# A conditioned two-layer trunk: four chunks of the conditioning product in a row, and VectorE's block transposes in place of selection matmuls

## The chip, the cores and the metric

One core of one Trainium2 chip runs the whole program. The metric is the time of one execution on the device in microseconds (us), as the median of several runs. The engines are TensorE (PE, with its weight loads PEld), VectorE (DVE), ScalarE (ACT), GpSimd (POOL) and SyncE (SP), which here only issues DMAs.

## What is computed

Two layers over 256 prompt tokens and 8 x 4 sample tokens of 1024 features. Each layer is a feed-forward, a mixer (a recurrence beside pooling) and a second feed-forward. All three are normalized and modulated by conditioning vectors, nine in number (one for the prompt, eight for the samples):

```python
mod = (jax.nn.silu(c) @ w_mod[l] + b_mod[l]).reshape(Bn, 3 * N_SUB, D_MODEL)[:, None]
u = _modnorm(x, norm_g[l, 0], mod[:, :, 0], mod[:, :, 1])     # rmsnorm(x, g) * (1 + scale) + shift
x = x + 0.5 * mod[:, :, 2] * _swiglu(u, w_ffn_in[l, 0], w_ffn_out[l, 0])
...
```

The mixer uses slots 3, 4 and 5 in the same way, the second feed-forward 6, 7 and 8.

`silu(c) @ w_mod[l]` is the conditioning product: 9 rows by 1024 by 9216 columns for each layer, 72 MB of weights in all. Its result is wanted with the features on the partitions: `mod[l]` is [128, 72 feature tiles, 9].

## The kernel before

Activations lie with the features on the partitions and 288 tokens on the free axis. A float32 product is three float32r passes, so a weight tile of 128x128 gives three matmuls of 288 columns (`mm3`, L243). Weights come from memory in slots of eight tiles (`load_slot`, L203, 512 KB, three buffers, issued on SP). Each half slot, a strip of four tiles, is split by ScalarE (`wh`, L224) and VectorE (`wl`, L225) into buffers for four strips. A feed-forward (`ffn`, L516) first makes 22 pairs of column tiles (gate and up, index j, 16 weight tiles each) and then 8 output tiles (22 weight tiles each). The first pairs behind a norm take a special form; `first_products` covers them.

The conditioning product is woven in between. A chunk is one load of 1 MB (`modw`, L292, SP's queue, five buffers). Its matmuls (L314) use four column tiles of TensorE at once: block q of the chunk's columns goes to partitions 32 q of a PSUM tile `psmd`, of which there is one buffer. A wide chunk holds 128 rows of `w_mod` for 4 x 512 columns. So a large group of 2048 columns takes eight chunks; the tail of each layer (1024 columns) takes four chunks, and the first layer's first 2048 columns are four small groups of two chunks each, in which a chunk holds 512 rows for 4 x 128 columns. `mod_step` (L296) carries out one chunk. `ffn` calls it at the head of every pair j from 3 or 4 on (L584) and behind every output tile (L600), with two loads ahead; below, such a place is called a tick. Groups 0 to 6 of layer 0 are opened at the program's start, 36 more chunks (layer 0's tail, layer 1's large groups) at the end of the first mixer, and layer 1's tail at the end of the second (L1299). `mod_close` flushes what is left at a mixer's head.

When a group is complete, ScalarE copies its PSUM rows to SBUF (L321). The next `mod_step` first calls `mod_cols` (L324): a matmul per 128 columns of `rows` against the constant `sel` (L334) brings the nine wanted rows of each block to the features' partitions, and VectorE adds the bias and finishes shifts, scales and gates (L341, L347, L351). These matmuls write `psmd` too (`pswk` for the small groups).

The order of instructions on each engine is set at build time by the framework's planner. It takes, of the instructions that its own model of time thinks ready, the one that was written first; blocks under `high_priority` (weight loads and splits) count as written 75 instructions earlier. The weight tiles' matmuls are tied to each other in their written order by `issue_after`; the conditioning product's matmuls are not, except in the first 48 weight tiles.

Of the kernel before, what the change touches and what calls it, by code (L numbers as in the profile page):

```python
# [25 lines left out]
P = 128  # L26
# [21 lines left out]
NV = NT + NC9 + 1  # even, as float32r asks  # L48
# [4 lines left out]
# w_in's column tiles in the order in which the mixer wants them: lora, k, r, v, gate lora, pool.  # L53
# [19 lines left out]
# behind a norm: pairs of column tiles (feed-forward) and column tiles (mixer) that don't wait for it  # L73
# [3 lines left out]
# w_mod's columns in groups of four blocks (one to a column tile of the tensor engine): the blocks'  # L77
# width and first columns. A chunk is one load of a group's rows. The first layer's first groups are
# the shifts and scales of two feature tiles each: its first products start behind them.
MODC = 2048  # L80
MOD_TAIL = [(256, [8192 + 256 * q for q in range(4)])]
MOD_GROUPS = [
    [(128, [256 * h + o for o in (0, 128, 1024, 1152)]) for h in range(4)]
    + [(512, [2048 * g + 512 * q for q in range(4)]) for g in range(1, 4)] + MOD_TAIL,
    [(512, [2048 * g + 512 * q for q in range(4)]) for g in range(4)] + MOD_TAIL,
]
MOD_CHUNKS = [[D * 4 * w // (P * MODC) for w, _ in g] for g in MOD_GROUPS]
# [100 lines left out]
class Kernel:  # L188
# [135 lines left out]
    def mod_cols(self):  # L324
        """Brings a finished group's rows to the features' partitions."""
        nc = self.nc
        if self.mod_rows is None:
            return
# [4 lines left out]
        for j in range(nj):  # L333
            nc.tensor.matmul(ps[:, 36 * j:36 * j + 36], rows[:, P * j:P * j + P], self.cst("sel"), start=True, stop=True)  # L334
# [1143 lines left out]
```

## Time and profile before

| | us |
|---|---|
| median of 3 runs | 1487.39 (1486.8 to 1488.97) |
| span of the profiled execution | 1486.2 |
| TensorE busy in it | 1438.0 |
| VectorE busy | 937.8 |
| ScalarE busy | 725.8 |

The profile is of one execution. Busy times are of the whole span, so they are averages over stages; matmuls are pipelined, so the distance between the starts of two of them tells more than the time given for one. In a chain of waits the program is followed back from its end to what released each step.

### The profile page before, as it was taken

Reading aid. Unit: us, or ns where it says so; the run is one execution under the profiler, and the core shown is the slowest. Engines: PE = TensorE matmul, PEld = TensorE weight load, DVE = VectorE, ACT = ScalarE, POOL = GpSimd, SP = SyncE. Lnnn points to the kernel's source line nnn. Section 1 sums busy time; section 2 is a strip of 40 time slices with the busy share of each in tenths; the row PEclk is TensorE's granted clock in tenths of the full one; section 3 lists DMA queues with packets and bytes.
Section 4 is the critical chain, followed back from the end, with each engine's and each line's share of the span. In section 5 each row is a group of like instructions: output and inputs, shape, how many; then the busy total and the mean of one; then the engine's idle time right before and its main releaser. Section 6 shows DMA issues by size and latency. Waiting matters only on the chain.

```text
span 1486.2 us, 30239 instructions
## 1 busy us (share of the span) xinstructions
PE 1438.0 (97%) x11944; PEld 1311.5 (88%) x11944; DVE 937.8 (63%) x1975; ACT 725.8 (49%) x1456; POOL 222.0 (15%) x320
## 2 busy tenths in 40 slices
PE   6999999999999989999999999999899999999997
PEld 5888899988778988888989899998887799999997
DVE  4544456798656885445567455668966678755554
ACT  4444444674434554444446445447653355645532
POOL 0000001153213130000111000121622213100011
PEclk9999999998999999999999999999999999999999
DMA  8888754443324657777775644443323356444442
GB/s 349 310 322 308 275 183 146 147 136 104 104 76 161 238 189 271 285 265 258 251 256 186 239 139 164 170 168 136 123 89 105 103 178 255 142 156 170 162 166 103
DMA packets 72383, 281.95 MB, mean 190 GB/s; under 512 B 9584, under 2 KB 11504, under 8 KB 62896
## 3 DMA queue, kind: packets, MB, share of 16 engines
q1 hardware_dynamic: 66384, 272.24, 51.3%
q10 hardware_dynamic: 5856, 7.78, 1.6%
q8 instruction: 93, 1.52, 0.4%
q14 instruction: 50, 0.41, 0.1%
HBM read 275.76 MB, written 4.23 MB: 188 GB/s over the span
## 4 chain that ended last, share of the span: by engine, by line
PE 83%; DVE 10%; issue 2%; DMA 1%; POOL 1%; ACT 1%; POOLq 0%; DVEq 0%; SPq 0%; ACTq 0%
PE psmm L250 41%; PE pswk L250 29%; PE psmd L314 4%; DVE wl L225 3%; DVE ul L474 1%; DVE xn L471 1%; DMA modw<-in_wmod 1%; POOL pw L669 1%; PE pswk L1128 1%; PE pswk L896 1%; PE psmd L334 0%; PE pswk L383 0%; PE pswk L1249 0%; DMA cc<-in_c 0%; PE pswk L1030 0%
## 5 line engine op out<-in xcount | busy, mean ns | idle before, releaser
L225 DVE TENSOR_TENSOR wl<-raw,wh 128x512 fp32r<-128x512 f32 x732 | 520.4, 714 | 411.6 <-ACT wh L224 402.4
L224 ACT CAST wh<-raw 128x512 fp32r<-128x512 f32 x732 | 452.1, 620 | 573.4 <-PE psmm L250 297.1
L250 PE MATMUL psmm<-uh,wh 128*128 128x288 f32 x1072 | 327.2, 305 | 1.1 <-ACT uh L482 1.1
L250 PE MATMUL psmm<-uh,wl 128*128 128x288 f32 x1072 | 319.1, 298 | 4.0 <-DVE wl L225 4.0
L250 PE MATMUL psmm<-ul,wh 128*128 128x288 f32 x1072 | 318.8, 297 | 0.1
L250 PEld LDWEIGHTS psmm<-uh,wh 128*128 128x128 f32 x1072 | 203.7, 190 | 34.4 <-ACT wh L224 19.5
L250 PEld LDWEIGHTS psmm<-uh,wl 128*128 128x128 f32 x1072 | 203.3, 190 | 9.8 <-DVE wl L225 5.1
L250 PEld LDWEIGHTS psmm<-ul,wh 128*128 128x128 f32 x1072 | 203.6, 190 | 2.7 <-issue 1.4
L250 PE MATMUL pswk<-uh,wh 128*128 128x288 f32 x608 | 182.0, 299 | 0.0
L250 PE MATMUL pswk<-ul,wh 128*128 128x288 f32 x608 | 179.9, 296 | 0.0
L250 PE MATMUL pswk<-uh,wl 128*128 128x288 f32 x608 | 179.8, 296 | 0.0
L370 POOL TENSOR_TENSOR sq<-x 128x288 f32<-128x288 f32 x42 | 30.4, 723 | 874.6 <-DVE x L510 866.5
L250 PEld LDWEIGHTS pswk<-uh,wh 128*128 128x128 f32 x608 | 114.7, 189 | 19.2 <-ACT wh L224 18.0
L250 PEld LDWEIGHTS pswk<-uh,wl 128*128 128x128 f32 x608 | 114.6, 189 | 1.7 <-issue 1.7
L250 PEld LDWEIGHTS pswk<-ul,wh 128*128 128x128 f32 x608 | 114.7, 189 | 0.8 <-issue 0.8
L250 PE MATMUL psmm<-hl,wh 128*128 128x288 f32 x352 | 104.0, 296 | 0.0
L250 PE MATMUL psmm<-hh,wh 128*128 128x288 f32 x352 | 104.0, 295 | 0.0
L250 PE MATMUL pswk<-hl,wh 128*128 128x288 f32 x352 | 103.9, 295 | 0.0
L250 PE MATMUL pswk<-hh,wh 128*128 128x288 f32 x352 | 103.9, 295 | 0.0
L250 PE MATMUL pswk<-hh,wl 128*128 128x288 f32 x352 | 103.8, 295 | 0.0
L250 PE MATMUL psmm<-hh,wl 128*128 128x288 f32 x352 | 103.8, 295 | 0.0
L314 PE MATMUL psmd<-modw,csilu 128*32 128x512 f32 (+2 forms) x832 | 79.0, 486 | 9.5 <-DMA modw<-in_wmod 9.5
(340 smaller groups left out, 2513.7 us busy)
## 6 DMA issues: line engine op xcount, KB each, us to landing
raw<-in_wflat SPq DMA_DIRECT2D x366, 512.0 KB, 3.3
modw<-in_wmod SPq DMA_DIRECT2D x72, 1024.0 KB, 5.6
s<-in_wkv ACTq DMA_DIRECT2D x16, 256.0 KB, 2.9
o_wkvs<-s SPq DMA_DIRECT2D x8, 256.0 KB, 2.5
x<-in_x SPq DMA_DIRECT2D x1, 1152.0 KB, 5.8
o_y<-yo SPq DMA_DIRECT2D x2, 288.0 KB, 2.4
o_y<-yo ACTq DMA_DIRECT2D x2, 288.0 KB, 2.6
o_pool<-po SPq DMA_DIRECT2D x8, 67.5 KB, 2.4
```

Of the source, the lines that this page charges most:

```text
L224: self.nc.scalar.copy(wh, src)
L225: self.nc.vector.tensor_tensor(out=wl, in0=src, in1=wh.bitcast(F32), op=ALU.subtract)
L250: self.last = self.nc.tensor.matmul(ps, w, x, start=start and n == 0, stop=stop and n == 2)
L314: mm = nc.tensor.matmul(self.mod_ps[32 * q:32 * q + 32, :size], self.csilu[:, k, :], w[:, kk, q, :], start=(k == 0), stop=(k == KD - 1))
L370: nc.gpsimd.tensor_tensor(out=t, in0=x, in1=x, op=ALU.mult)
L471: nc.vector.scalar_tensor_tensor(out=t, in0=self.x[:, k, :TP], scalar=g1, in1=r[:, :TP], op0=ALU.mult, op1=ALU.mult)
L474: nc.vector.scalar_tensor_tensor(out=ul, in0=t, scalar=s[:, k, 0:1], in1=uh.bitcast(F32), op0=ALU.add, op1=ALU.subtract)
L669: G.tensor_tensor(out=nx[:, lo:], in0=cur[:, lo:], in1=cur[:, lo - d:PEXT - d], op=ALU.add)
L896: T.transpose(ps[:n, 128 * hp:128 * hp + 128], src(hp), ident)
L1128: T.matmul(ps[halves[e], :], BKTs[halves[e], hp, :], uv[halves[e]].rearrange("p b v -> p (b v)"), start=True, stop=True)
```

## The change

Four things are done. First, the feed-forward's ticks call `mod_tick`: it carries out four chunks one behind the other once four of a group are loaded (`MOD_RUN`), and otherwise none; each tick asks for one more load. Second, the columns of `w_mod` are packed differently on the host, before the launch: block q of a group now holds the q-th 32 features of each of the group's feature tiles. Third, `mod_cols` has no matmul: VectorE transposes the group's PSUM tile in blocks of 32x32 straight into `rows`, which puts the 128 features of each tile on the partitions, and the bias is added from there. It is called directly behind a group's last chunk. Fourth, ScalarE's copy and the constant `sel` are gone. Comments and docstrings are left out of the new file.

```diff
 MODC = 2048
-MOD_TAIL = [(256, [8192 + 256 * q for q in range(4)])]
+MOD_BUFS, MOD_RUN = 5, 4
 MOD_GROUPS = [
-    [(128, [256 * h + o for o in (0, 128, 1024, 1152)]) for h in range(4)]
-    + [(512, [2048 * g + 512 * q for q in range(4)]) for g in range(1, 4)] + MOD_TAIL,
-    [(512, [2048 * g + 512 * q for q in range(4)]) for g in range(4)] + MOD_TAIL,
+    [[2 * h + o for o in (0, 1, 8, 9)] for h in range(4)]
+    + [list(range(16 * g, 16 * g + 16)) for g in range(1, 4)] + [list(range(64, 72))],
+    [list(range(16 * g, 16 * g + 16)) for g in range(4)] + [list(range(64, 72))],
 ]
...
     def mod_step(self, n=1):
         nc = self.nc
         for _ in range(n):
-            self.mod_cols()
             if self.mod_at == len(self.mod_todo):
                 return
-            self.mod_load(int(self.mod_ahead == 0))
+            self.mod_load(int(self.mod_ahead == 0 and self.mod_next == self.mod_at))
...
             self.mod_load()
             if nk * (c + 1) == KD:
-                rows = self.p_rows.tile([P, 512], F32, tag="rows", name="rows")
-                nc.scalar.copy(rows[:, :size], self.mod_ps[:, :size])
-                self.mod_rows = rows, l, size, starts
-
-    def mod_cols(self):
-        """Brings a finished group's rows to the features' partitions."""
+                self.mod_cols(l, tiles, size)
+
+    def mod_tick(self):
+
+        if self.mod_at == len(self.mod_todo):
+            return
+        l, g, c = self.mod_todo[self.mod_at]
+        n = min(MOD_RUN, MOD_CHUNKS[l][g] - c)
+        if self.mod_next - self.mod_at >= n:
+            self.mod_ahead = 0
+            self.mod_step(n)
+        self.mod_ahead = self.mod_next - self.mod_at
+        self.mod_load(1)
+
+    def mod_cols(self, l, tiles, size):
+
         nc = self.nc
...
-        nj = size // P
-        ps = self.ps_wk() if nj == 1 else self.p_md.tile([P, 512], F32, tag="md", name="psmd")
-        for j in range(nj):
-            nc.tensor.matmul(ps[:, 36 * j:36 * j + 36], rows[:, P * j:P * j + P], self.cst("sel"), start=True, stop=True)
-        pv = ps[:, :36 * nj].rearrange("p (j q c) -> p q j c", j=nj, q=4)
...
+        rows = self.p_rows.tile([P, 512], F32, tag="rows", name="rows")
+        nc.vector.transpose(rows[:, :size], self.mod_ps[:, :size])
+        rows = rows[:, :size].rearrange("p (m r) -> p m r", r=32)
+        n = 0
+        while n < len(tiles):
+            o = tiles[n]
+            w = 1
+            while n + w < len(tiles) and tiles[n + w] == o + w and (o + w) % KD:
+                w += 1
+            m = self.mod[l][:, o:o + w, :]
             b = POFF["b_mod"][0] + o
...
+            nc.vector.tensor_tensor(out=m, in0=rows[:, n:n + w, :NC9], in1=b, op=ALU.add)
             slot = o // KD
...
                 if not pre:
                     if j == PRE_F and not start:
                         self.v_cm.__exit__(None, None, None)
-                    self.mod_ahead = max(self.mod_ahead, 2)
-                    self.mod_step()
+                    self.mod_tick()
...
                 self.residual(l, 2 if f == 0 else 8, m, ps)
-                self.mod_step()
...
+                self.mod_tick()
```

## Rows read from the trace of the kernel before

**Rows 1.** Page: busy us (share) and instructions of each engine; engines' shares of the chain.
```profile
PE 1438.0 (97%) x11944; PEld 1311.5 (88%) x11944; DVE 937.8 (63%) x1975; ACT 725.8 (49%) x1456; POOL 222.0 (15%) x320
...
PE 83%; DVE 10%; issue 2%; DMA 1%; POOL 1%; ACT 1%; POOLq 0%; DVEq 0%; SPq 0%; ACTq 0%
```

**Rows 2.** Windows: busy time in 50 to 120 us, in the columns of its head line.
```profile
core 0: us, PE busy (x) PEld busy (x) DVE busy (x) ACT busy (x) POOL busy (x), PEclk, DMA share, GB/s
...
50.00:120.00 70.00, 70.00 (x525) 60.47 (x518) 34.65 (x64) 30.70 (x60) 0.00 (x0) 1.00 0.89 330
```

**Rows 3.** Chain of waits, 50 to 125 us: start, us, what.
```profile
49.59 0.99 PE psmd L314 x8
...
57.13 0.99 PE psmd L314 x8
...
110.72 1.93 PE psmm L250 x14
112.66 1.00 PE psmd L314 x8
```

**Rows 4.** Chain of waits, an output tile of the third feed-forward.
```profile
941.67 8.73 PE psmm L250 x66
```

**Rows 5.** Timeline of TensorE, 118.0 to 119.6 us: start, us, instruction.
```profile
118.05 0.29 PE L250 MATMUL pswk<-uh,wl 128*128 128x288 f32 x1
118.27 1.07 PE L314 MATMUL psmd<-modw,csilu 128*32 128x512 f32 x8
119.27 0.40 PE L250 MATMUL psmm<-uh,wh 128*128 128x288 f32 x1
119.50 0.30 PE L250 MATMUL psmm<-ul,wh 128*128 128x288 f32 x1
```

**Rows 6.** Timeline of TensorE at the start: one narrow chunk, and two in a row.
```profile
25.71 1.08 PE L314 MATMUL psmd<-modw,csilu 128*32 128x128 f32 x32
...
37.53 1.96 PE L314 MATMUL psmd<-modw,csilu 128*32 128x128 f32 x64
```

**Rows 7.** Instructions by line, L314 and L334: records, ns min/median/max, first and last start.
```profile
L314 PE MATMUL psmd<-modw,csilu x832: 272/592/618, 9.5 to 1309.5; 128*32 128x512 f32 x89, 128*32 128x128 f32 x52, 128*32 128x256 f32 x26
...
L334 PE MATMUL psmd<-consts,rows x64: 195/279/280, 109.7 to 1316.6; 128*128 128x36 f32 x64
```

**Rows 8.** Timeline of TensorE around the selection behind a large group.
```profile
109.61 0.30 PE L250 MATMUL pswk<-uh,wl 128*128 128x288 f32 x1
...
110.56 0.38 PE L250 MATMUL psmm<-uh,wh 128*128 128x288 f32 x1
110.78 0.29 PE L250 MATMUL psmm<-ul,wh 128*128 128x288 f32 x1
```

**Rows 9.** Instructions by line: a block transpose of VectorE in the mixer, SBUF to SBUF.
```profile
L1165 DVE STREAM_TRANSPOSE Tc<-Gd x2: 711/712/714, 374.4 to 1105.7; 128x512 f32<-128x512 f32 x2
```

**Rows 10.** Page, costliest groups: busy us, mean ns, idle before and its releaser.
```profile
L225 DVE TENSOR_TENSOR wl<-raw,wh 128x512 fp32r<-128x512 f32 x732 | 520.4, 714 | 411.6 <-ACT wh L224 402.4
```

**Rows 11.** Timelines of TensorE and of SP's queue around one chunk.
```profile
140.89 1.07 PE L314 MATMUL psmd<-modw,csilu 128*32 128x512 f32 x8
...
142.02 0.33 SPq L292 DMA_DIRECT2D modw<-in_wmod  x1
```

**Rows 12.** Windows: a stretch in which the DMA engines are saturated (share, GB/s last).
```profile
54.00:57.00 3.00, 3.00 (x24) 2.89 (x22) 1.39 (x2) 1.41 (x3) 0.00 (x0) 1.00 1.03 421
```

**Rows 13.** Page, DMA issues: count, KB each, median us from issue to landing.
```profile
raw<-in_wflat SPq DMA_DIRECT2D x366, 512.0 KB, 3.3
modw<-in_wmod SPq DMA_DIRECT2D x72, 1024.0 KB, 5.6
```

**Rows 14.** Timelines of ScalarE and VectorE at the start, 9 to 22 us.
```profile
18.30 0.40 ACT L400 COPY rb<-pswk 128x288 f32<-128x288 f32 x1 [0.61 <-PE pswk L397]
...
19.52 0.48 DVE L471 SCALAR_TENSOR_TENSOR xn<-x,mod,rb 128x256 f32<-128x256 f32 x1
```

**Rows 15.** Timeline of TensorE at the start, around the second group's selection.
```profile
29.08 0.30 PE L250 MATMUL pswk<-uh,wl 128*128 128x288 f32 x1
...
31.95 0.40 PE L250 MATMUL psmm<-uh,wh 128*128 128x288 f32 x1 [0.54 <-ACT uh L482]
32.47 0.40 PE L250 MATMUL psmm<-ul,wh 128*128 128x288 f32 x1
```

More of the change, by code (lines that the diff above doesn't have):

```diff
@@ L137 @@
 NPAR = _o
-CONSTS = [("ones", 1), ("sel", 36), ("eps", 1), ("ident", 128), ("mhalf", 1), ("hs", 32), ("hb", 128),
+CONSTS = [("ones", 1), ("eps", 1), ("ident", 128), ("mhalf", 1), ("hs", 32), ("hb", 128),
           ("maskp", 128), ("masks", 64), ("bmask", 8), ("id32", 32), ("id16", 16), ("halves", 2), ("scan", 288),
@@ L175, in make_consts @@
     put("halves", (p % 32 // 16)[:, None] == np.arange(2))
-    sel = (p // 32)[:, None, None] == np.arange(4)[None, :, None]
-    put("sel", sel & ((p % 32)[:, None, None] == np.arange(NC9)[None, None, :]))
     sc = np.ones(NT, np.float32)
@@ L305, in mod_step @@
             self.mod_at += 1
-            size, starts = MOD_GROUPS[l][g]
+            tiles = MOD_GROUPS[l][g]
+            size = 32 * len(tiles)
             nk = MODC // (4 * size)
@@ L319, in mod_step @@
             if nk * (c + 1) == KD:
-                rows = self.p_rows.tile([P, 512], F32, tag="rows", name="rows")
-                nc.scalar.copy(rows[:, :size], self.mod_ps[:, :size])
-                self.mod_rows = rows, l, size, starts
-    def mod_cols(self):
-        nc = self.nc
-        if self.mod_rows is None:
-            return
-        rows, l, size, starts = self.mod_rows
-        self.mod_rows = None
-        nj = size // P
-        ps = self.ps_wk() if nj == 1 else self.p_md.tile([P, 512], F32, tag="md", name="psmd")
-        for j in range(nj):
-            nc.tensor.matmul(ps[:, 36 * j:36 * j + 36], rows[:, P * j:P * j + P], self.cst("sel"), start=True, stop=True)
-        pv = ps[:, :36 * nj].rearrange("p (j q c) -> p q j c", j=nj, q=4)
-        for h in range(2):
-            o = starts[2 * h] // P
-            m = self.mod[l][:, o:o + 2 * nj, :]
+                self.mod_cols(l, tiles, size)
[10 more added lines that the diff above has]
+    def mod_cols(self, l, tiles, size):
+        nc = self.nc
+        rows = self.p_rows.tile([P, 512], F32, tag="rows", name="rows")
[8 more added lines that the diff above has]
+            m = self.mod[l][:, o:o + w, :]
             b = POFF["b_mod"][0] + o
-            b = self.params[l][:, b:b + 2 * nj].rearrange("p (q j) -> p q j", q=2)
-            nc.vector.tensor_tensor(out=m.rearrange("p (q j) c -> p q j c", q=2), in0=pv[:, 2 * h:2 * h + 2],
-                                    in1=b.unsqueeze(3).to_broadcast([P, 2, nj, NC9]), op=ALU.add)
+            b = self.params[l][:, b:b + w].unsqueeze(2).to_broadcast([P, w, NC9])
+            nc.vector.tensor_tensor(out=m, in0=rows[:, n:n + w, :NC9], in1=b, op=ALU.add)
             slot = o // KD
@@ L345, in mod_cols @@
                 g = POFF["norm_g"][0] + 8 * (slot // 3) + o % KD
-                g = self.params[l][:, g:g + 2 * nj]
                 nc.vector.scalar_tensor_tensor(
-                    out=m, in0=m, scalar=1.0, in1=g.unsqueeze(2).to_broadcast([P, 2 * nj, NC9]),
+                    out=m, in0=m, scalar=1.0, in1=self.params[l][:, g:g + w].unsqueeze(2).to_broadcast([P, w, NC9]),
                     op0=ALU.add, op1=ALU.mult)
@@ L351, in mod_cols @@
                 nc.vector.tensor_scalar(m, m, 0.5, None, op0=ALU.mult)
+            n += w
     def mod_close(self):
@@ L554, in ffn @@
                 self.rms_spread()
-                self.mod_cols()
                 self.u_open()
@@ L1298, in mixer @@
         es.close()
-        self.mod_open(5, mod_chunks(l, 7 - 3 * l) + (mod_chunks(1, 0, 1, 2, 3) if l == 0 else []), 0)
+        self.mod_open(MOD_BUFS, mod_chunks(l, 7 - 3 * l) + (mod_chunks(1, 0, 1, 2, 3) if l == 0 else []), 0)
         self.pre_open(l, 2)
@@ L1419, in pack @@
     for l in range(DEPTH):
-        for w, starts in MOD_GROUPS[l]:
-            a = np.stack([d["w_mod"][l][:, c:c + w] for c in starts], 1).reshape(D * 4 * w // (P * MODC), -1, P, 4 * w)
+        for tiles in MOD_GROUPS[l]:
+            w = 32 * len(tiles)
+            a = d["w_mod"][l].reshape(D, 72, 4, 32)[:, tiles].transpose(0, 2, 1, 3)
+            a = a.reshape(D * 4 * w // (P * MODC), -1, P, 4 * w)
             wm.append(a.transpose(0, 2, 1, 3).reshape(-1, P, MODC))
```

7 lines of the change are left out of this document (2 added, 5 removed).

## The prediction

> **What bounds the kernel now.** Read the page's busy shares and its chain first. TensorE is busy for 97% of the span and stands for 83% of the chain that ended last; VectorE is at 63%, ScalarE at 49% [rows 1]. That is an average, so next comes the stage in which the conditioning chunks run: from 50 to 120 us TensorE is busy all the time at full granted clock, VectorE half of the time, and the DMA engines for 0.89 of it [rows 2]. The chain inside that stage repeats with a period of 7.54 us, from one chunk at 49.59 to the next at 57.13 [rows 3]. Between two chunks stand two column tiles of 24 weight-tile matmuls each. Where no chunk comes between, 66 of them take 8.73 us, so 0.1323 us each [rows 4]; 48 take 6.35 us, and the other 1.19 us of the period are the chunk. So in these stages a microsecond taken off TensorE's queue is a microsecond off the kernel, as long as nothing else becomes late; in the stage of rows 4 TensorE already runs without chunks at 0.1323 us a matmul and nothing is late there.
>
> **The change part by part.** The sum is made against the profiled execution, span 1486.2 us; the median of the three runs is 1487.39 us, 1.2 us more, and I carry that 1.2 us over.
>
> *Merged visits.* One chunk alone: the weight-tile matmul before it starts at 118.05, the next at 119.27 and the one after at 119.50 [rows 5]. That is 1.22 + 0.23 us where two steps of 0.132 would stand, so a visit costs 1.22 + 0.23 - 0.26 = 1.19 us, as the period said. Two chunks in a row occur only at the start, in the narrow form (four times as many matmuls with a quarter of the columns). One narrow chunk of 32 records takes 1.08 us, as long as the wide one's 1.07 [rows 5]; two in a row, 64 records, take 1.96 [rows 6]. So the second costs 0.88 us, and each chunk that follows another directly saves 1.19 - 0.88 = 0.31 us (bounds 0.29 and 0.33, by the rounding of the starts). How many do so? 832 records [rows 7] are 72 chunks: 8 narrow ones of 32 records at the start (unchanged in order), 56 wide ones of 8 and 8 of the tails with 16; the last 64 now go in runs of four, since every large group has 8 chunks and both tails have 4, and a run never passes a group's end. That is 16 runs, 48 merged visits: 48 x 0.31 = 14.9 us.
>
> Do the runs find their ticks? A tick (one per column pair from j = 3 or 4 on, one per output tile) loads one chunk and runs four once four are loaded. The first feed-forward has 19 + 8 = 27 ticks; runs fall on 5, 9, 13, 17, 21 and 25, so its 24 chunks are done, and the shift and scale of the mixer (second group) are there at tick 17, before they are read behind tick 19. In the next two feed-forwards two chunks are loaded ahead, runs fall on ticks 3, 7, ... 35 of 52; the next layer's first group is done at 11, before 18. Nothing is left for the flush at the mixer's head.
>
> *Selection matmuls.* At a large group's end: 109.61 to 110.56 and 110.78 [rows 8], 0.95 + 0.22 - 0.26 = 0.91 us on TensorE. The 64 records behind the start [rows 7] are seven large groups of 8 and two tails of 4: 7 x 0.91 + 2 x 0.45 = 7.3 us, all in stages where TensorE is the bound. They go without a successor on TensorE.
>
> *The transpose instead.* ScalarE's copy of the rows disappears, which is worth nothing since ScalarE waits anyway. VectorE gets 13 block transposes. The trace has none that reads PSUM; the nearest row is one from SBUF of the same 128x512, 0.71 us [rows 9]. The adds behind it read SBUF instead of PSUM, in the same number. Per large group VectorE's queue gets some 0.7 us longer; behind it in that queue stand the splits that TensorE needs. TensorE has four split strips ready, 4 x 12 x 0.132 = 6.35 us, and they fill up while a run keeps it busy. So I cost it at 0 on the path. Bounds: nothing below 0, since ScalarE, which is relieved, stands for 1% of the chain [rows 1]; above, all of it exposed, 7 x 0.71 + 2 x 0.36 + 4 x 0.18 = 6.4 us (the smaller ones estimated by their columns). I take 0, because the cover of 6.35 us is nine times the instruction.
>
> The Trainium skill speaks against this step: "TensorEngine Tiling", section "PSUM Bottleneck", says that column tiling speeds up the products but not the emptying of PSUM, and to use both ScalarE and VectorE for it. Here one bank is emptied after eight chunks and next written three ticks later (at the start sooner), which speaks against a need; by the rule the sum would lose the exposed bound, which is the third rival.
>
> *Loads.* The same 72 loads go out on SP's queue, past the weight loads there. Before, a load is issued as soon as a buffer is free: 142.02, directly behind the chunk that started at 140.89 and lasted 1.07 [rows 11]; so the planner pulls loads forward as far as the five buffers let it, whatever tick they are written in. After a run four buffers come free within its 1.19 + 3 x 0.88 = 3.83 us, so I expect four loads of 1 MB in a burst. Saturated, the DMA engines moved 421 GB/s [rows 12]: 1.05 MB / 421 GB/s = 2.5 us a load, 10 us for the burst. What is queued behind it are weight slots; a slot's load lies three slots of two strips ahead, and its buffer is freed when strips four ahead of TensorE are split, so a load is out about 8 strips x 1.59 = 12.7 us before use, less one strip's copy and subtraction, an estimate of twice the 0.71 us of the subtraction [rows 10]: 11.3 us. A slot's load takes 3.3 us [rows 13]; behind the whole burst 13.3, which would be 2 us late, but TensorE takes no weights during the run, which adds 3.83 us of cover. Cost 0, with 1.8 us in hand; what it costs if that cover is gone is the first rival. Over four ticks the demand is 8.4 MB in 4 x 6.35 + 3.83 = 29.2 us, 287 GB/s against 421.
>
> *Start.* The first products wait for the first shifts and scales. VectorE's first normalization starts at 19.52, behind the adds on the selected columns, though the spread 1/rms was there at 18.70 [rows 14]: without the copy and the selection up to 0.8 us sooner. At 29.08 the next product waits until 31.95, then 0.52 us more [rows 15]; the two chunks in between cost 1.19 + 0.88 and two steps 0.26, so 2.87 + 0.52 - 2.33 = 1.1 us is the wait behind the second group's selection, which sat in TensorE's queue behind a stretch of weight-tile matmuls. The transpose follows the group directly, so that goes. Two more small selections of two records, 0.91 / 4 each: 0.5 us. Together 2.4 us (bounds 0.5, if VectorE's splits get in front of the transposes, and 2.9).
>
> Sum: 14.9 + 7.3 + 2.4 = 24.6 us. Span 1486.2 - 24.6 = 1461.6, and with 1.2 us 1462.8 us.
>
> **The rivals.**
> 1. *Weights behind the burst (slower).* If the four loads go out later than the run, say behind the weight loads that already wait on SP, the run's 3.83 us of cover don't count and each burst makes TensorE wait 2 us. It decides from 1.8 us of delay on. With 2 us in each of 16 runs, 32 us are lost against 24.6 gained: 1487.4 + 7.4 = 1495. For it: loads leave at once when a buffer is free [rows 11] and the engines are at 0.89 in this stage already [rows 2]. Against: the buffers come free during the run, and a mean of 287 GB/s is far below 421.
> 2. *The run is broken up (the change doesn't do what it says).* The chunks' matmuls are tied to each other by no order; the planner may put weight tiles in between where it thinks a chunk's load has not landed. Before, the first chunk behind each group's end stands 14 matmuls further back than the others [rows 3]. All broken: 1462.8 + 14.9 = 1478; one break per run: 16 x 0.31 = 5.0, so 1468.
> 3. *Emptying PSUM by VectorE alone binds*, 6.4 us: 1469. For it: a single bank. Against: three ticks between a group's end and the next run.
> 4. *The last chunk's load is late.* It is written one tick, 6.35 us, ahead of its run and takes 5.6 us [rows 13], plus up to two weight slots in front of it (2.5 us): up to 1.8 us in 16 runs, 1463 to 1491; middle 1477. Against: loads are pulled forward as far as the buffers go [rows 11].
>
> **How the numbers follow.** Forecast 0.73, rival 1 0.05, rival 2 0.11, rival 3 0.06, rival 4 0.05. The predicted time is the forecast's, 1462.8. Its own range goes by the bounds: 48 x 0.29 + 7.3 + 0.5 = 21.7 to 48 x 0.33 + 7.3 + 2.9 = 26.0, so 1461.4 to 1465.7; an estimate of 2 us for a shifted order of work elsewhere goes on each side: 1460 to 1468. To leave out no more than 2 in 10 I reach to rival 3 and the mild half of rival 2: 1459 to 1474. What this kernel's measurement can tell from no change is 0.2%, 3 us. Faster holds the forecast, rivals 2 and 3 and most of 4: 0.92; within 0.2% 0.02; slower, rival 1 and the worst of 4: 0.06.
>
> **What would show each step.** Right: in the feed-forwards the chain shows 32 records of the conditioning product together with about 3.8 us every fourth tick and weight-tile matmuls 0.132 us apart in between; no record of the selection; 13 transposes near 0.7 us with nobody on TensorE waiting for them; no wait at 31.95's place. Wrong: groups of 8 or 16 records (rival 2); TensorE or ScalarE's split waiting for the weight slots some 8 to 14 us behind a run (rival 1); the run's first or fourth chunk waiting for VectorE or for its own DMA (rivals 3, 4). The prediction is wrong if a merged chunk costs much more than 0.88 us, which rests on pairs of the narrow form.

## The result, and the profile after

The changed kernel takes 1466.88 us, the median of four runs (1462.14 to 1476.75), against 1487.1 us before (1485.76 to 1488.97, four runs beside them): a ratio of 0.9866, 95% interval 0.9843 to 0.9889. Forecast were 1462.8 us in a range of 1459 to 1474. The profiled execution has a span of 1466.4 us, 19.8 less than the 1486.2 of before; forecast were 24.6 less. So the sign and the range held, and some 4 to 5 us of the gain went somewhere that the sum did not have.

The page of the changed kernel: busy times, the chain's shares, the load queue for instructions (packets, MB, share), the splits, and two DMA rows (count, KB, us to landing).

```profile
PE 1416.2 (97%) x11872; PEld 1307.7 (89%) x11872; DVE 945.6 (64%) x1984; ACT 719.8 (49%) x1443; POOL 225.0 (15%) x320
...
q8 instruction: 93, 1.52, 0.4%
...
PE 83%; DVE 11%; issue 3%; POOL 1%; ACT 1%; DMA 1%; POOLq 0%; DVEq 0%; ACTq 0%
...
L225 DVE TENSOR_TENSOR wl<-raw,wh 128x512 fp32r<-128x512 f32 x732 | 522.0, 717 | 365.7 <-ACT wh L224 352.5
...
raw<-in_wflat SPq DMA_DIRECT2D x366, 512.0 KB, 3.4
modw<-in_wmod SPq DMA_DIRECT2D x72, 1024.0 KB, 7.2
```

Against [rows 1, 10, 13]: TensorE has 72 matmul records less and 21.8 us less to do, VectorE 7.8 us more. TensorE stands for the same 83% of the chain; "issue" rose from 2% to 3%, which will matter below. A chunk's load takes 7.2 us to land where it took 5.6, since four go out together; a weight slot's takes 3.4, where it took 3.3.

The stage that the prediction read, 50 to 120 us, in the columns of [rows 2] (start:end, length, busy us of PE, PEld, DVE, ACT and POOL with instructions, granted clock, DMA share, GB/s):

```profile
50.00:120.00 70.00, 70.00 (x539) 64.41 (x538) 37.10 (x67) 31.99 (x61) 0.00 (x0) 1.00 0.84 307
```

TensorE is still the bound there, and gets through 539 records instead of 525 in the same 70 us. What it does with them is seen in the timeline of TensorE around one run (start, us, engine, line, instruction, count):

```profile
101.93 0.29 PE L250 MATMUL pswk<-uh,wl 128*128 128x288 f32 x1
102.15 3.64 PE L314 MATMUL psmd<-modw,csilu 128*32 128x512 f32 x32
105.72 0.40 PE L250 MATMUL psmm<-uh,wh 128*128 128x288 f32 x1
105.97 0.29 PE L250 MATMUL psmm<-ul,wh 128*128 128x288 f32 x1
```

32 records of the conditioning product in one piece: 3.79 us from the weight tile before to the one after, and 0.25 to the next, where two steps of 0.132 would stand: 3.77 us a run. All 16 runs look like this (the tails with 64 records, 3.82 in one piece). Four single chunks cost 4 x 1.19 = 4.76, so a run saves 0.99 us.

The transposes, by line (count, ns min/median/max, first and last start, shapes):

```profile
L338 DVE STREAM_TRANSPOSE rows<-psmd x13: 310/716/717, 16.6 to 1284.3; 128x512 f32<-128x512 f32 x7, 128x128 f32<-128x128 f32 x4, 128x256 f32<-128x256 f32 x2
```

Thirteen of them, 0.716 us for the large ones, against 0.712 of the one from SBUF in [rows 9]. No instruction waits for them, and no selection matmul is left.

Where in the program the time went is read by comparing the start of the same weight tile in both profiled executions (worked out from the two traces):

| weight tile | before, us | after, us | difference |
|---|---|---|---|
| first | 21.26 | 20.56 | -0.69 |
| 49th, end of the start | 50.52 | 47.52 | -3.00 |
| first of the first mixer | 271.15 | 260.56 | -10.60 |
| first behind the first mixer | 522.97 | 512.05 | -10.92 |
| first of the second layer | 775.21 | 753.75 | -21.46 |
| 41st of the second mixer | 1021.46 | 997.39 | -24.07 |
| 217th of the second mixer | 1155.63 | 1137.34 | **-18.30** |
| first behind the second mixer | 1254.27 | 1235.96 | -18.30 |
| last | 1475.03 | 1455.25 | -19.78 |

Up to the second mixer 24.07 us are gained, about what was forecast. Then, in a stretch that the change does not touch (from the 41st to the 217th weight tile of the mixer, called its main part below), 5.77 us are lost, and not won back. The experiments ask what the terms are worth one by one, and what happens there.

One row of this table is not what it seems. At the start the two executions do not run at the same pace. Two neighbouring products of before, then of after:

```profile
22.18 0.44 PE L250 MATMUL psmm<-uh,wl 128*128 128x288 f32 x1
22.42 0.44 PE L250 MATMUL pswk<-uh,wh 128*128 128x288 f32 x1
...
21.32 0.30 PE L250 MATMUL psmm<-uh,wl 128*128 128x288 f32 x1
21.46 0.29 PE L250 MATMUL pswk<-uh,wh 128*128 128x288 f32 x1
```

In the profile of before, products stand 0.24 us apart up to 25.1 us, in that of after 0.13 to 0.14 from the third product on. So part of the 3.00 us at the 49th tile is a difference of executions and not of kernels; the start is taken up again below with profiles of like pace.

### The profile page after: what moved, and what is told of

The parts are those of the page before. It is cut to its first block, busy times and chain, and to the rows that moved or that the text cites. A ratio compares the mean times of both kernels' runs of the same rounds, so it can differ in the third digit from the quotient of the medians.

```text
span 1466.4 us, 30086 instructions
## 1 busy us (share of the span) xinstructions
PE 1416.2 (97%) x11872; PEld 1307.7 (89%) x11872; DVE 945.6 (64%) x1984; ACT 719.8 (49%) x1443; POOL 225.0 (15%) x320
## 4 chain that ended last, share of the span: by engine, by line
PE 83%; DVE 11%; issue 3%; POOL 1%; ACT 1%; DMA 1%; POOLq 0%; DVEq 0%; ACTq 0%
PE psmm L250 41%; PE pswk L250 29%; PE psmd L314 4%; DVE wl L225 3%; DVE ul L480 1%; DVE xn L477 1%; PE pswk L889 1%; POOL pw L672 1%; PE pswk L899 1%; PE pswk L1131 1%; PE pswk L389 1%; PE pswk L1252 0%; DMA cc<-in_c 0%; PE pswk L1033 0%; PE pswk L1111 0%
## 5 line engine op out<-in xcount | busy, mean ns | idle before, releaser
L225 DVE TENSOR_TENSOR wl<-raw,wh 128x512 fp32r<-128x512 f32 x732 | 522.0, 717 | 365.7 <-ACT wh L224 352.5
L314 PE MATMUL psmd<-modw,csilu 128*32 128x512 f32 (+2 forms) x832 | 69.1, 480 | 9.5 <-DMA modw<-in_wmod 9.5
```

Of the source, the lines that this page charges most:

```text
L225: self.nc.vector.tensor_tensor(out=wl, in0=src, in1=wh.bitcast(F32), op=ALU.subtract)
L314: mm = nc.tensor.matmul(self.mod_ps[32 * q:32 * q + 32, :size], self.csilu[:, k, :], w[:, kk, q, :], start=(k == 0), stop=(k == KD - 1))
```

## The experiments

**The kernel again, and the change in parts.** Four kernels on one chip: the changed kernel once more; it without the runs (one chunk a tick, two loads ahead, as before, but with the transposes); the kernel before with the runs alone (copy and selection kept); and the changed kernel with runs of two.

```diff
 # without the runs, in mod_tick
-        n = min(MOD_RUN, MOD_CHUNKS[l][g] - c)
...
+        self.mod_step()
 # runs alone: mod_tick goes into the kernel before and begins with its selection
+    def mod_tick(self):
+        self.mod_cols()
...
 # runs of two
-MOD_BUFS, MOD_RUN = 5, 4
+MOD_BUFS, MOD_RUN = 5, 2
```

> The changed kernel as it is, five more rounds. Theory A (the forecast's mechanism is whole, and what is missing is TensorE's clock in the second mixer): the profiled execution of the change gained 24.0 us up to the second mixer and gave 5.8 us back there at half the granted clock; so its runs lie on one line of time over mean granted clock, about 1.1 us for each 0.001, and a run at 0.995 takes 1462 us, one at 0.982 about 1476 us. The kernel before, which is tight at 1486 to 1489, stays tight. Theory B (something in the feed-forwards varies, weights behind the burst of loads): runs spread at the same granted clock, and the profile shows gaps between weight-tile matmuls of the feed-forwards outside the runs of four.

> The transpose alone: one chunk at each tick with two loads ahead, as before, but VectorE's transpose and adds in place of ScalarE's copy and the selection. If the sum's terms are separate: 7 x 0.91 + 2 x 0.45 = 7.3 us of selection and some 2 us at the start are gained, 64 visits still cost 1.19 us each: 1487 - 9 = 1478 us, ratio 0.994. If the transpose is what makes VectorE or TensorE late (rival 3 of the prediction), less than 5 us are gained. If the spread of the changed kernel comes with the transpose, it shows here too.

> Runs of four alone: ScalarE's copy, the selection matmuls and their place one tick behind a group stay as before. If the terms are separate: 16 runs at 3.77 us in place of 64 visits at 1.19 us, 76.2 - 60.3 = 15.9 us gained: 1471 us, ratio 0.989. The start stays as before. If runs of four only pay because the selection is gone, the gain is under 10 us.

> The changed kernel with runs of two in place of four (one number). If what is saved goes by visits: 32 runs of two at 1.19 + 0.86 = 2.05 us, 65.6 us, against 16 at 3.77, 60.3 us: 5.3 us slower than the changed kernel at the same granted clock, 1466 to 1468 us where the clock is 0.995. If the burst of four loads costs something, runs of two are less than 3 us slower or even faster.

| kernel | median, us (runs) | ratio to before, interval | at the second mixer's 41st tile | at the last tile |
|---|---|---|---|---|
| changed, again | 1468.78 (1464.75 to 1473.66) | 0.9875, 0.9853 to 0.9896 | -23.79 | -22.97 |
| transposes, no runs | 1484.43 (1482.01 to 1495.16) | 0.9987, 0.9970 to 1.0004 | -8.70 | +0.98 |
| runs, no transposes | 1473.92 (1471.89 to 1474.8) | 0.9908, 0.9893 to 0.9924 | -14.40 | -13.84 |
| runs of two | 1472.98 (1467.31 to 1475.63) | 0.9900, 0.9878 to 0.9922 | -18.00 | -16.66 |

The last two columns are differences to the profile of before, as in the table above. The two parts add: 8.70 + 14.40 = 23.1 against the 24.07 of both. Of the 8.70, 1.03 lie in the start and 0.86 in the first mixer; the other 6.8 are what seven large selections and one tail's should give, 7 x 0.91 + 0.45. Runs of two are the dose between. In their timeline of TensorE a pair stands like this:

```profile
60.77 0.29 PE L250 MATMUL pswk<-uh,wl 128*128 128x288 f32 x1
60.99 1.92 PE L314 MATMUL psmd<-modw,csilu 128*32 128x512 f32 x16
62.85 0.40 PE L250 MATMUL psmm<-uh,wh 128*128 128x288 f32 x1
63.09 0.29 PE L250 MATMUL psmm<-ul,wh 128*128 128x288 f32 x1
```

62.85 - 60.77 + 0.24 - 0.26 = 2.06 us, so the second chunk costs 2.06 - 1.19 = 0.87, and the three that follow in a run of four (3.77 - 1.19) / 3 = 0.86. The whole times don't show this as clearly as the fourth column. The transposes alone are 8.70 us ahead at the second mixer and 3.45 us in the median; in their profiled execution 8.64 us were lost again in the second mixer's main part. The changed kernel's nine runs lie between 1462.1 and 1476.8. So the loss does not lie in a stage that the change works on, and it differs from execution to execution.

**The new hole at the start.** By the table the start gained 1.8 us, not 2.4 (3.00 less the 1.19 of one chunk that moved from the start into a run). But most of this is the pace. In four profiles products stand 0.24 us apart up to 24.5 to 25.1 us: that of before, that of the kernel before with a filled hole in the mixers (see below) and two of the changed kernel with such a fill, whose start is the changed kernel's. In them the 49th tile starts at 50.52 and 50.32, against 49.13 and 48.95. That is 1.4 us in the mean, so the start itself gained about 0.2. In the changed kernel's timeline of TensorE (a bracket gives the idle time and what ended it) a hole stands that before did not have:

```profile
41.00 0.29 PE L250 MATMUL pswk<-uh,wl 128*128 128x288 f32 x1
42.06 0.40 PE L250 MATMUL psmm<-uh,wh 128*128 128x288 f32 x1 [0.77 <-ACT uh L488]
42.78 0.40 PE L250 MATMUL psmm<-ul,wh 128*128 128x288 f32 x1 [0.32 <-DVE ul L489]
```

VectorE's timeline says why:

```profile
37.41 0.48 DVE L477 SCALAR_TENSOR_TENSOR xn<-x,mod,rb 128x256 f32<-128x256 f32 x1
37.80 1.29 DVE L225 TENSOR_TENSOR wl<-raw,wh 128x512 fp32r<-128x512 f32 x2
39.01 0.48 DVE L480 SCALAR_TENSOR_TENSOR ul<-xn,mod,uh 128x256 fp32r<-128x256 f32 x1
39.40 0.69 DVE L225 TENSOR_TENSOR wl<-raw,wh 128x512 fp32r<-128x512 f32 x1
...
40.14 0.48 DVE L477 SCALAR_TENSOR_TENSOR xn<-x,mod,rb 128x256 f32<-128x256 f32 x1
40.54 0.69 DVE L225 TENSOR_TENSOR wl<-raw,wh 128x512 fp32r<-128x512 f32 x1
```

Three splits (L225) were put between the two normalizations (L477) whose second half TensorE needs next. The experiment gives the start's normalization a priority ahead of the splits:

```diff
-                        self.sample_scale(l, sub, k, k + 2, nc.vector)
-                        self.u(l, sub, k, k + 2)
+                        with self.tc.high_priority(offset=2 * PRIO):
+                            self.sample_scale(l, sub, k, k + 2, nc.vector)
+                            self.u(l, sub, k, k + 2)
```

> The changed kernel with the normalization of the start put ahead of the weight splits in VectorE's order (the two steps of each pair of tiles at 37.4 to 41.3 of the profile after come before the splits that stood between them). TensorE's order is the same. Theory: the stall of the start at 41.0 (holes of 1.06 and 0.72 us between weight tiles) was these splits; the holes shrink to 0.3 us or less in sum and the feed-forward behind is 1.1 to 1.5 us earlier, seen stage by stage, so a time of about 1466 where the changed kernel gives 1467 to 1469, less than the scatter that the clock leaves. Rival: the late splits now stop TensorE a few tiles later (wait for wl at 42 to 46), and nothing is gained or up to 1 us lost.

Measured: 1464.9 us (1460.4 to 1474.46, ratio 0.9858, 0.9831 to 0.9885). At the 49th weight tile the profile is 2.40 us ahead of the changed kernel's, 2.0 of them gained since the first (both have products 0.13 us apart from the start on); the holes at 41.0 and the 0.52 at 29.02 are gone. VectorE now goes from one normalization to the other in 0.53 us:

```profile
36.60 0.48 DVE L477 SCALAR_TENSOR_TENSOR xn<-x,mod,rb 128x256 f32<-128x256 f32 x1
37.00 0.22 DVE L485 TENSOR_TENSOR xs<-xs,rb 128x64 f32<-128x64 f32 x1
37.13 0.48 DVE L477 SCALAR_TENSOR_TENSOR xn<-x,mod,rb 128x256 f32<-128x256 f32 x1
```

So the theory held, and its size was above the 1.1 to 1.5 expected. The whole time can't show it, since the runs scatter over 14 us. At like pace, the changed kernel with a filled hole and the mended start has its 49th tile at 47.04, so with the mend the start gains some 2.2 us.

**What happens in the mixer.** First the granted clock (0.50 is the lower level, 1.2 GHz; 1.00 is 2.4 GHz). TensorE's windows in the changed kernel's second mixer (start:end, length, busy us and records, granted clock, DMA share, GB/s):

```profile
1044.00:1046.00 2.00, 1.08 (x9) 1.00 0.83 253
1046.00:1048.00 2.00, 2.00 (x19) 0.86 0.15 48
1048.00:1050.00 2.00, 2.00 (x13) 0.50 0.70 258
```

Behind a place where TensorE was busy 1.08 of 2 us, in the middle of the score products (K against Q of the recurrence), the clock falls to one half. Weight-tile products then start 0.24 us apart, as in this timeline from a later such stretch, against 0.132:

```profile
1072.32 0.45 PE L250 MATMUL psmm<-ul,wh 128*128 128x288 f32 x1
1072.56 0.45 PE L250 MATMUL psmm<-uh,wl 128*128 128x288 f32 x1
```

The second mixer's main part had 17.1 us at half clock in the profile of after and 3.4 in that of before. My theory was that the hole in the score products lets the clock fall, so the next experiment fills it with nine products of 128x288 that nobody reads. Two more kernels fill a second hole (2.4 us, TensorE waits for VectorE's pooled difference) and a third (between the 32x32 products that join the blocks of an inverse).

```diff
+    def warm(self, n, after=None):
+        t = self.p_md.tile([P, 512], F32, tag="md", name="warm")
+        for _ in range(n):
...
+                    after = self.nc.tensor.matmul(t[:, :NT], self.uh[:, 0, :P], self.uh[:, 1, :], start=True, stop=True)
...
         for i in range(2):
             for q in range(2):
                 for e in range(2):
                     scores(e, i, q)
+            if i == 0:
+                self.warm(9)
```

> The changed kernel with nine products of 128x288 added in each mixer, whose result nobody reads, between the fourth and the fifth of the eight score groups, where TensorE stood still for 1.19 us (323.8 to 326.0 in the first mixer, 1043.83 to 1045.02 in the second of the profile after). They need 9 x 0.13 = 1.2 us, which is what the hole holds; the order of everything else on TensorE stays. Theory: the hole is what lets the granted clock fall behind it (half for 6.8 us from 327.2 and 6.8 us from 1047.4). With it filled these two stretches are at full clock; the weight tiles in them take 0.13 us a product instead of 0.24, which gives back some 2 to 3 us a mixer: 1461 to 1465 us against 1467 to 1469 of the changed kernel, granted clock of the whole 0.993 or more. Rival: the clock falls for another reason (the thin products themselves, or a place that moves from execution to execution); then the low stretches stay or move and the time stays at 1466 to 1470.

> As the run before, and 18 more such products in each mixer ahead of the product that waits 2.4 us for the pooled difference (348.9 to 351.6 and 1068.45 to 1071.12 of the profile after). With them some of the 32x32 joins behind stand elsewhere in TensorE's order. Theory of the clock: all low stretches but that of the joins vanish, 1459 to 1463 us, granted clock 0.995 or more. Rival: the added products are paid where the wait is shorter than they are, up to 2 x 2.3 us, and the clock falls at the joins as before: 1467 to 1474 us.

> As the run before, and eight and six more such products between the groups of 32x32 joins of each mixer, where TensorE stood 1.2 to 1.8 us. Theory of the clock: no stretch of a mixer at half clock is left but for the last microseconds of the kernel, granted clock 0.996 or more, at most 1.8 us a mixer paid for products that do not fit: 1458 to 1463 us. Rival: 1467 to 1475 us, the products cost time and the clock falls elsewhere.

| fill | median, us (runs) | ratio, interval | us at half clock in the main parts, first and second mixer |
|---|---|---|---|
| none (changed kernel, nine runs) | 1468.2 (1462.1 to 1476.8) | 0.9866, 0.9843 to 0.9889 in the first four | 10.2 and 17.1; 6.8 and 6.8 |
| scores | 1462.18 (1461.13 to 1463.52) | 0.9834, 0.9817 to 0.9850 | 3.4 and 3.4 |
| scores and pooled difference | 1463.18 (1461.93 to 1465.09) | 0.9842, 0.9824 to 0.9859 | 3.4 and 3.4 |
| all three | 1469.89 (1465.48 to 1471.09) | 0.9876, 0.9857 to 0.9894 | 0 and 0 |

One filled hole brings the time to the forecast's 1462.8 and takes the scatter from 14.6 us to 2.4. The second brings nothing more. With all three no stretch of the mixers' main parts is at half clock, but the main parts are longer than with one fill (133.9 and 135.2 us, against 132.2 and 133.3): the products added at the joins are paid for, and some joins stand elsewhere in TensorE's order. 1469.89. So the clock is not all. The reading of TensorE's waits shows a second thing that the fill changed. In the changed kernel (who waited for whom: total us, times, longest):

```profile
PE psmm L250 <- DVE wl L225: 5.1, 6, 1.7
...
PE pswk L1164 <- issue: 3.9, 3, 1.6
```

and in the kernel before:

```profile
PE psmm L250 <- DVE wl L225: 5.0, 6, 1.7
...
PE pswk L1161 <- issue: 1.2, 1, 1.2
...
PE pswk L896 <- issue: 0.6, 1, 0.6
```

The waits for the weights (first rows) are the same. But at the joins (L1161 before, L1164 after; L896 are transposes between them) TensorE waits 3.9 us instead of 1.8 for something the profile shows only as "issue"; in the first profile with the filled scores no such row is left, in a second one 0.9 us. In the changed kernel's timeline of TensorE:

```profile
1076.95 1.29 PE L1155 MATMUL pswk<-GT,Off 32*32 32x32 f32 x128
...
1079.16 0.24 PE L1164 MATMUL pswk<-Gd,O 32*32 32x32 f32 x3
1080.98 0.52 PE L1164 MATMUL pswk<-Gd,O 32*32 32x32 f32 x38 [1.58 <-issue]
...
1085.00 0.21 PE L1164 MATMUL pswk<-Gd,O 32*32 32x32 f32 x1 [1.23 <-issue]
```

128 small products pass in 1.29 us, then TensorE stands for 1.58, and again for 1.23. In five profiles (the changed kernel twice, and those with the start mended, with runs of two and with the transposes alone) both waits of the second mixer stand behind the same records, the 3rd and the 127th of the 128 of L1164. Between them lie 124 of these products and four transposes (L899), with a weight load each: 256 instructions. The page's queue of instructions moved 93 loads, and TensorE executed 2 x 11872 = 23744 instructions: 255 for each load. In the trace such loads of 16 KB begin at 1078.10 and at 1082.62, for 1.43 and 0.96 us, and TensorE goes on 1.45 and 1.42 us behind their ends. So I read these as waits for TensorE's own instructions, which come in blocks; where a block ends depends on how many instructions stand ahead. In the kernel before, the wait stands behind the 63rd record of its L1161.

Counting bears this out. All 27 waits of TensorE that the 14 profiles put down to "issue" begin at the same place of a block of 256 (behind 193 to 196, counted over products and weight loads from the first), and each ends 0.9 to 1.6 us behind the end of a load of 16 KB. The places follow from the edits, too. The change takes 68 selection products, with a weight load each, from ahead of the second mixer: 63 + 68 = 131, which is the 127th record and the four transposes. A filled hole adds 9 products in each mixer, 18 up to there: 127 - 18 = 109, and in the three profiles with this fill and such a wait (two with 288 columns, one with the 8 of the next kernel) the wait stands behind the 109th. In the kernel before with the fill it stands behind the 45th, 63 - 18. So the removal of the selection moved the block ends. That brought a second wait: in the changed kernel one more end falls into the joins, at 1077.04, behind the 8th record of L1155, and the next load begins only at 1078.10. With the fill this end falls into the weight tiles ahead of the joins (1073.1 in the second profile of the fill), the load for it has begun at 1071.24, and the wait at the 3rd record is gone.

**Place or clock.** That parts into two theories, which the filled hole had changed together. The next kernel adds the same nine instructions at the same place with 8 columns instead of 288 (only the arguments of its two calls are shown):

```diff
-    t[:, :NT], self.uh[:, 0, :P], self.uh[:, 1, :]
+    t[:, :8], self.uh[:, 0, :P], self.uh[:, 1, :8]
```

> The changed kernel with the same nine unread products at the same place of each mixer, but of 8 columns instead of 288: as many instructions, and the hole between the score groups stays nearly as empty as it was (nine of them are over in some 0.5 of the 1.19 us, and stream 72 columns instead of 2592). It parts two things that the full fill changed together: the stretches at half clock behind the scores were gone, and the waits at the 32x32 joins that the trace puts down to issue fell from 3.4 to 4.1 us (in four profiles of kernels with runs) to 0 and 0.9 us. Theory of the clock: the granted clock falls behind the scores as in the changed kernel (6.8 us from about 327 and, in some executions, about 1047), and the time is 1464 to 1470 with a scatter of 5 us or more; of the fill's gain only what comes from the issue waits is left, if these are short here. Rival, the place of the instructions alone: the issue waits are short (1.3 us or less) and the time is 1461 to 1463.5 with a scatter of some 3 us, as with the full fill, the stretch at half clock behind the scores or not.

Measured: 1462.0 us (1461.08 to 1463.66, ratio 0.9826, 0.9813 to 0.9839). The rival won. TensorE's waits in it:

```profile
PE pswk L1175 <- issue: 0.8, 2, 0.5
```

The main parts of the mixers, in windows of the four kernels with the columns of [rows 2]. Before, first and second mixer:

```profile
289.00:424.00 135.00, 127.59 (x1434) 108.16 (x1433) 105.18 (x277) 76.18 (x166) 48.00 (x75) 0.96 0.32 107
1021.00:1156.00 135.00, 125.83 (x1433) 106.36 (x1432) 105.45 (x277) 76.59 (x165) 47.87 (x75) 0.99 0.32 107
```

After:

```profile
279.00:413.00 134.00, 126.00 (x1429) 106.99 (x1429) 104.59 (x275) 75.69 (x164) 47.84 (x75) 0.96 0.33 107
997.00:1137.00 140.00, 130.32 (x1430) 109.86 (x1429) 104.64 (x275) 75.89 (x164) 47.75 (x75) 0.94 0.31 103
```

After with the scores filled by 288 columns (a second job of that kernel):

```profile
280.00:413.00 133.00, 125.42 (x1442) 107.10 (x1441) 105.93 (x276) 76.14 (x166) 48.02 (x75) 0.99 0.34 109
998.00:1131.00 133.00, 124.83 (x1439) 105.46 (x1438) 105.56 (x276) 76.56 (x165) 48.06 (x75) 1.00 0.34 108
```

After with 8 columns:

```profile
281.00:415.00 134.00, 127.64 (x1439) 108.27 (x1438) 104.59 (x275) 75.92 (x164) 47.94 (x75) 0.96 0.34 108
999.00:1132.00 133.00, 124.99 (x1441) 105.92 (x1439) 105.95 (x276) 76.18 (x165) 48.13 (x75) 1.00 0.33 108
```

The windows are rounded to whole microseconds; the lengths below are exact. The first mixers tell the fill's effect on the clock: with 8 columns it falls behind the scores as before (0.96), with 288 it does not (0.99). That is worth 133.8 - 132.5 = 1.3 us. In all six profiles with the 288 columns the clock stays up there, in eight without it falls in seven; in the profile with the start mended it stays up without any fill.

The second mixers tell the place of the instructions. The changed kernel's 140 us (139.95) are the longest of three profiles of its order, so here are all 14 (us, worked out from the traces; the third column counts stretches that begin 0.6 to 1.4 us behind the end of a wait for "issue"):

| second mixer's main part | waits for "issue" | at half clock | of it right behind such a wait | length |
|---|---|---|---|---|
| before | 1.2 | 3.4 | 0 | 134.2 |
| before, filled | 1.1 | 3.4 | 0 | 134.2 |
| runs, no transposes | 1.1 | 10.2 | 0 | 135.8 |
| transposes, no runs | 2.7 | 20.5 | 17.1 | 142.8 |
| runs of two | 3.0 | 6.8 | 6.8 | 136.7 |
| changed; again; start mended | 2.8; 3.0; 3.0 | 17.1; 6.8; 6.8 | 6.8; 6.8; 6.8 | 139.9; 136.5; 137.0 |
| scores filled; again; 8 columns; filled and start mended | 0; 0.7; 0.5; 0.9 | 3.4; 0; 0; 0 | 0 | 133.3; 132.7; 132.5; 133.0 |
| two holes filled; three | 0; 0 | 3.4; 0 | 0 | 134.4; 135.2 |

Wherever the waits come to 2.7 us or more, the clock falls right behind one of them; in the nine with 1.2 or less it never does there. So the half clock behind the joins goes with the waits, but no run changed one without the other. The rest of the changed kernel's half clock is something else: its stretches at 1047.4 (6.8 us, behind the scores) and 1071.3 (3.4, behind the wait for the pooled difference) come before the first of the waits, which begins at 1079.40, and the two other profiles of this order don't have them. With a fill, wide or thin, the length goes from 137.8 in the mean of three to 132.9 in the mean of four, by shorter waits and by less time at half clock.

The expectation was wrong in one more point. The nine thin products were to be over in 0.5 us; they took as long as the wide ones:

```profile
1046.32 0.27 PE L338 MATMUL warm<-uh 128*128 128x8 f32 x1
1046.45 1.03 PE L341 MATMUL warm<-uh 128*128 128x8 f32 x8
```

0.13 us apart, with a 128x128 weight load each. The hole was thus filled in time, with 72 columns instead of 2592.

**The same fill in the kernel before, and both edits together.** On one chip: the fill of 288 columns in the kernel before; again in the changed kernel; and the changed kernel with the fill and the mended start.

> The kernel before with the same nine unread products in the score groups' hole of each mixer, the order of its TensorE otherwise kept. If the missing part of the forecast (24.6 us forecast, 18 to 21 measured) went to stretches of half clock that the changed kernel draws more often, then with the hole filled in both the difference is that of the feed-forwards and the start: the changed kernel with the fill (1462.2) stands 22 to 24 us below this one, so this one comes out at 1484 to 1487, near its own 1487. Rival: the fill is worth as much to the kernel before as to the changed one (5 to 6 us): 1481 to 1482, and the difference stays at 19 to 20 us.

> The changed kernel with the fill of the score groups again, beside the two runs above on the same chip: 1461 to 1464 us, scatter of some 3 us. If the small scatter of its first job was luck, it is 8 us or more, as of the changed kernel.

> The changed kernel with both edits that moved time: the start's normalization ahead of the weight splits (2.0 us up to the 48th weight tile in the run of that alone) and nine unread products in the hole of the score groups of each mixer (1462.2 us median alone, 1461.1 to 1463.5). If both are what they seem, they add: 1459 to 1461 us, scatter of some 3 us. Rival: the start's gain was a draw of the clock (its run alone lay between 1460.4 and 1474.5): 1461 to 1464.

| kernel | median, us (runs) | ratio to before, interval |
|---|---|---|
| before, filled | 1484.76 (1483.9 to 1493.01) | 0.9992, 0.9976 to 1.0009 |
| changed, filled | 1461.63 (1460.85 to 1463.05) | 0.9829, 0.9815 to 0.9842 |
| changed, filled, start mended | 1459.76 (1459.55 to 1463.35) | 0.9821, 0.9807 to 0.9835 |

The fill is worth little to the kernel before (2.6 us in the medians, its interval holds no change), and some 6 to the changed one. In the profile of before with the fill the gain lies in the first mixer's main part: 134.3 us with 10.2 at half clock became 131.1 with none. Two of its eleven runs took 1491.7 and 1493.0, so the fill does not end the scatter everywhere. With it in both, the change is worth 1484.76 - 1461.63 = 23.1 us. The terms as measured come to the same: 15.8 for the runs, 7.3 for the selection and 0.2 for the start are 23.3. The mended start adds 1.9 (in the medians; the intervals of the two overlap). The last kernel is 27.6 us below the kernel before and the best of all that ran.

## Why the forecast was near, and what it missed

- *Merged visits*: right, and slightly too small. A following chunk costs 0.86 us, forecast 0.88 from pairs of the narrow form [rows 6]; 16 runs save 16 x 0.99 = 15.8 us, forecast 14.9. The runs were kept whole, and fell on ticks as counted. Rival 2 did not occur.
- *Selection matmuls*: 7.3 us as forecast. The transposes alone gave 6.8 where 6.8 were due.
- *Transpose at 0*: right. 0.716 us, and nobody waits, so rival 3 did not occur. The Trainium skill's "TensorEngine Tiling (Array Packing)", section "PSUM Bottleneck", says that the copy out of PSUM may become the bottleneck behind tiling, and to use both ScalarE and VectorE for it. This case shows no need of that: with VectorE alone TensorE's waits for VectorE's splits (`psmm` behind `wl`) are 5.1 us, where they were 5.0.
- *Loads at 0*: right. The chunks' loads land later (7.2 us for 5.6), as a burst of four should, weight slots do not (3.4 for 3.3), and the waits for weights are unchanged. Rivals 1 and 4 did not occur.
- *Start*: 2.4 forecast, about 0.2 measured at like pace; the 1.8 of the two first profiles was mostly luck of the execution. The waits named did shrink (the first product is 0.69 us earlier; the 2.87 us ahead of 31.95 in [rows 15] are 2.11 ahead of 29.02, and the 0.52 behind them stayed). What failed is that the gain was taken without asking what VectorE does next: with shifts and scales earlier, its splits came between two normalizations, which cost 1.5 us at 41.0. The lower bound of 0.5 named splits that get in front, but ahead of the transposes. Mended, the start gains 2.0 us more, and with that what was forecast.
- *The rest of the program at no change*: this is the step that failed, and it had no sentence of its own. "An estimate of 2 us for a shifted order of work elsewhere" was all the range had for it. In the first two profiles 25.5 us are gained outside it (24.07 up to the second mixer, 1.48 behind it, the start's pace included); the second mixer's main part gave back 5.77. Worked out: the waits for instructions there were 2.8 us instead of 1.2, and 17.1 us instead of 3.4 were at half clock. From the first mixers a microsecond at half clock costs 0.30 us (131.1 us with none in two profiles, 134.1 in the mean of six with 10.2). That makes 1.6 + 0.30 x 13.7 = 5.7. The two other profiles of this order lost 2.3 and 2.8 us there: the waits are the steady part, the half clock varies.

So the mechanism of the two large terms was right. Their sum came close in part by luck, since the runs were taken 0.9 us too small and the start 2.2 too large. The missing part was the place of TensorE's waits for instructions, in a part of the program that was not touched, and the half clock that goes with them or comes by itself. In the trace of before the waits show as "issue" at the joins, and a count of the products that the change takes away would have told where they go. The Trainium skill, "Runtime: NRT & Kernel Launch", section "Instruction fetch mechanics", says that instructions come in blocks of 16 KiB, 256 of them, and that crossing a block's end is mostly hidden. The trace agrees with the size (255 instructions for each load) and with the rule in the feed-forwards, where no such wait stands; at the joins it does not, with 1.58 us in one crossing.

What stays open: whether the half clock behind the joins comes from the waits, and what lets the clock fall in one execution and not in the next. Neither was tried by itself.

## What to carry to other kernels

Where a second kind of product interrupts TensorE's main stream, price the visit and the content apart: here 0.33 of 1.19 us were the visit, and running four in a row saved three visits of four. When instructions are taken out of or added to a long program, look at places with many tiny products behind it, and at waits for "issue" there; a few instructions more or less can move microseconds, and counting them tells where to. When measured times of one kernel scatter by more than the effect, compare the starts of the same instruction stage by stage, and only between profiles whose clock is alike in that stage: here the start's term was 1.8 us by the first pair of profiles and 0.2 by pairs of like pace.

## What the runs showed of the hardware that was not expected

- Nine products of 128x8, each with its own 128x128 weights, take as long as nine of 128x288: 1.2 us, 0.13 us apart.
- A block transpose of 128x512 float32 costs VectorE the same from PSUM (0.716 us) as from SBUF (0.712).
- TensorE's granted clock went to half in the mixers for 0 to 20.5 us of a main part of some 135, mostly behind places where the engine had stood still for 1 to 2.4 us, though not each time; the same program differed between executions (6.8 to 17.1 us in the second mixer of the changed kernel), and its time by up to 14 us.
- TensorE waited up to 1.8 us at the end of a block of 256 of its own instructions where 256 pass in 2 to 3 us (27 waits in 14 profiles, each ending 0.9 to 1.6 us behind the end of a 16 KB load); in the feed-forwards, where they take some 16 us, there is no such wait.
